# Squared ReLU of an MLP's first product: which engines do it

## The chip, the cores and the metric

The kernel runs on one core of a Trainium2 chip. The metric is the device time of one execution in microseconds, lower is better. A core has five engines that run side by side, each through its own instructions in order: TensorE (PE; PEld is its loading of weights), VectorE (DVE), ScalarE (ACT), GpSimd (POOL) and SyncE (SP), whose queue here issues all loads and stores. An instruction waits until what it needs is there, and everything behind it on its engine waits too.

## The reference, cut to what matters

Two layers of a flow-matching backbone run over 1,152 tokens (1,024 grid tokens and 128 context tokens) of 1,024 features. Each layer has a group of mixers with one output projection, and then an MLP of 4,096 hidden features:

```python
h2 = rms_norm(x, p['norm2']) * (1 + sc2) + sh2
x = x + g2 * (jnp.square(jax.nn.relu(h2 @ p['w1'])) @ p['w2'])
```

The vectors sc2, sh2 and g2 come from a modulation of the condition vectors, `silu(cond) @ w_mod + b_mod`, which each layer has for itself. All is float32.

## The kernel before, in words

Features lie on partitions, tokens in the free dimension. Products are made in two float32r parts (a high part, rounded, and the rest), by three matmuls for each pair of tiles, lines 1081 to 1083. The MLP's two products are done by blocks, two by two, with seven products in place of eight (Strassen and Winograd). Tokens are cut into four blocks of 288 (`BLK`), two for each half `q`; the hidden features are cut into 16 pairs `j` of tiles. One call of `Line.add` is one product of blocks of the first MLP product: 16 pairs by 2 halves make 32 of them a layer. Each is seven runs of 12 matmuls of 128x288, 84 in all.

`Line.products` writes the runs into PSUM banks. Run 0 goes into `bA`, which ScalarE copies into a bank `bB`. Run 1 goes into `bE`, which ScalarE copies to SBUF as `s5` (the trace calls it `s`). Run 2 is added into `bB`, which is copied into a bank `bC`. Run 3 is added into `bA`, which gives block c11; run 4 into `bB`, which gives c22; run 5 into `bC`, which gives c12; run 6 into `bB` again, which gives c21. So run 6 may start only when c22 has been read out of `bB`. `Line.add` weaves the last three runs of one product under the first four of the next: 0, 4 of the one before, 1, 5 of the one before, 2, 6 of the one before, 3.

What becomes of the four blocks is in `hidden`. The functions `c1` (c11 and c21) and `c2` (c22 and c12, to which `s5` is still to be added) take each block out of PSUM into a tile `hr`, square the positive part, and `keep` stores it to DRAM (`hd`), from where the second product loads it. `s5` and `hr` are from one pool of five buffers. The helpers `act` (line 208, ScalarE), `ptt` (190, GpSimd), `vtt` (193, VectorE) and `vstt` (205, VectorE) issue one instruction each, so the trace shows their lines.

The left operands are made as they are needed, by `Weights.version`: VectorE forms sums of weight tiles (`wl`, lines 187 and 193), ScalarE rounds them (`ws`, line 181), and GpSimd, or VectorE for some, takes the rest (`ws`, lines 184 and 187). A ring holds seven such tiles, and one is made when one is free.

In the first layer VectorE also makes the modulation vectors of the second (`mod_tile`, line 270): 48 tiles, with six reductions each, emitted after the steps 6 to 31 of the first MLP product (`MLP_MODS`). Their operands `wm` are loaded by SyncE's queue.

The instructions of each engine are put in order by a planner that simulates the program when it is built (`schedule_with_timeline_sim=True`). An order on paper is thus also a result of the costs that this simulation gives to each instruction, which are not those of the chip.

Of the kernel before, what the change touches and what calls it, by code (L numbers as in the profile page):

```python
# [42 lines left out]
# a block of tokens: a quarter of the grid and one of the context  # L43
# [16 lines left out]
def weave(main, n_main, side, n_side):  # L60
    """Emits two streams evenly interleaved, by their numbers of steps."""
    done = [0, 0]
    gens = [main, side]
    n = [max(n_main, 1), max(n_side, 1)]
    live = [True, True]
    while live[0] or live[1]:
        i = 0 if live[0] and (not live[1] or done[0] * n[1] <= done[1] * n[0]) else 1
        try:
            next(gens[i])
            done[i] += 1  # L70
        except StopIteration:
            live[i] = False


def weave_steps(main, n_main, side, n_side):
    """The main stream, with the steps of a side stream spread over its own."""
    done = 0
    for i in range(n_main):
        if next(main, END) is END:
            return  # L80
        while done * n_main < (i + 1) * n_side and next(side, END) is not END:
            done += 1
        yield
    yield from main


def weave_at(main, side, counts):
    """The main stream, with the given number of steps of a side stream after each of its own."""
    for n in counts:
        next(main, END)  # L90
        run_out(take(side, n))
    run_out(main)
# [6 lines left out]
def steps(n, span, i):  # L99
    """How many of n steps fall on i when they are spread over a span."""  # L100
    a, b = (n * min(max(i + e - span[0], 0), span[1] - span[0]) // (span[1] - span[0]) for e in range(2))
    return b - a
# [15 lines left out]
def build(ctx, tc, I, O):  # L118
# [9 lines left out]
    def urgent(gen, offset):  # L128
        """A stream whose instructions go before those around it."""
        while True:  # L130
            with tc.high_priority(offset):
                step = next(gen, END)
            if step is END:
                return
            yield step

    # pools that come and go
# [20 lines left out]
    def phase(st, tag, bufs, w=NW, side="left"):  # L158
        """A pool of [128, w] tiles for one phase of a layer."""
        pool = st.enter_context(tc.tile_pool(name=tag, bufs=bufs, side=side, reuse_waits="tile"))  # L160
        return lambda name, dt=F32: pool.tile([P, w], dt, tag=tag, name=name)

    def two_phases(st, tag, n1, n2, w):
        """The same in two places, by turns n1 and n2 tiles."""
# [72 lines left out]
    # the early columns apart from the others, which come later  # L237
# [18 lines left out]
    # adaLN vectors, feature on partitions: mod[l][:, j, cond]  # L256
# [3 lines left out]
    def mod_tile(l, j, piece):  # L260
        """mod[l][:, j] from the rows of w_mod's transpose, in pieces."""
# [19 lines left out]
    def segs(n):  # L281
        # (lo, hi, cond) within chunk n
        if n < NCH - 1:
            return [(0, NW, 0)]
        return [(0, NW - TP, 0), (NW - TP, NW, 1)]

    def rms_sums(xs, n, alone=False):
        """The sums over the feature tiles of the squares of chunk n."""
# [14 lines left out]
    def rms_scale(sq, ps, w=P):  # L303
        """1/rms of 3w tokens, to be turned."""
# [11 lines left out]
    def rms_turn(R, ps, w=P):  # L316
        """1/rms of 3w tokens on all partitions, in SBUF."""
# [16 lines left out]
    class HT:  # L334
        """Normalised and modulated activations in two float32r parts, [k][n]."""
# [49 lines left out]
    def weight(src):  # L385
        """The float32r parts of a [128, 8, 128] weight tile, as functions of its k."""
        p = [half(src, i) for i in range(2)]
        return tuple((lambda k, j=j: p[k // 4][j][:, ti(k % 4)]) for j in range(2))
# [15 lines left out]
    def project_tokens(l, group, ht, evac, s_):  # L404
        """256 features projected with the tokens on partitions, 128 tokens a step."""
# [16 lines left out]
    def store_mix(t, dst, n, g_):  # L422
        """The float32r parts of a chunk of 128 features of the mixers' output, to DRAM."""
# [7 lines left out]
    class B:  # L431
        """The arrays of one pair of heads, in chunks of 384 tokens."""
# [23 lines left out]
    # where the first layer's later modulation vectors are computed, of 32  # L456
    MODS = (10, 11, 11, 0)
    # the projections under the recurrences of the heads
# [5 lines left out]
    class HGRN:  # L464
        """The recurrence of one pair of heads.

        levels(g): the scores of chunk g's three blocks of 128 tokens, by the levels of a binary tree;
        tail(g): its state updates, and all but the backward states' part of its output;
        back(): the backward states, their part of the output and its norm, in reversed order.
        """  # L470
# [205 lines left out]
    def hgrns(pairs):  # L676
        """Both pairs of heads: the end of each part runs under the levels of the next."""
# [10 lines left out]
    RG_STEPS = 1 + 2 * 7  # L688

    def rglru(l, i, xa, gel, gw, ud, g_):  # L690
# [13 lines left out]
        # each function of ScalarE for both directions at once  # L704
# [53 lines left out]
    def split_q(ps, n, h_t, l_t, sub):  # L758
        # queries in the order (row half, column block, row, column) and scaled
# [20 lines left out]
    def qk_project(l, p, win, ht, qd, kd, s_, ns=range(NCH)):  # L780
# [9 lines left out]
        def evac_k(n, ps):  # L790
            # the grid's rows in pairs, by columns
# [12 lines left out]
    # the grid's upper half for all pairs of heads, then the context's tokens and the lower half  # L804
# [4 lines left out]
    # where the output projection is done, by the tokens' half: of the first features, of the last  # L809
# [3 lines left out]
    def attention(l, qd, kd, vd, pool, out):  # L813
        """All query tiles of the four pairs of heads.

        Yields once the first pair's operands are under way, then after each tile the one that is complete.
        """
# [169 lines left out]
    class Ends:  # L987
        """What becomes of the fifth product and of the four blocks of a product of blocks."""
# [4 lines left out]
    def lo_subs(n):  # L993
        """The engines of a version's seven subtractions, n of them on VectorE."""
        return iter([vsub if (i + 1) * n // 7 > i * n // 7 else psub for i in range(7)])

    class Weights:
        """The left operands of the seven products, version by version, in the order of their use."""
# [56 lines left out]
    class Line:  # L1055
        """Products of blocks one after the other, the end of each under the start of the next."""
# [53 lines left out]
    def pieces(b):  # L1110
        """Block b of tokens by chunks and conditions: (chunk, from, to, condition, place in the block)."""
# [4 lines left out]
    def half_of(q, t, d, load):  # L1116
        """Moves blocks 2q and 2q + 1 of a [128, 2 * BLK] tile from or to DRAM."""
# [14 lines left out]
    def load_blocks(srcs, q, new):  # L1132
        """Blocks 2q and 2q + 1 of two tiles of features."""
# [12 lines left out]
    def blocks_of(t):  # L1146
        """The two blocks of a tile, and both."""
        return [t[:, c * BLK:(c + 1) * BLK] for c in range(2)] + [t]

    def load_half(src, q, new):  # L1150
        """Blocks 2q and 2q + 1 of a tile of features."""
# [15 lines left out]
    class NormOperands:  # L1167
        """The right operands of the seven products, from the features 2i and 2i + 1 of half q of the tokens.

        The steps take 2, 4, 4 and 4 places of [128, 2, BLK] (the second after the first, the fourth after the  # L1170
        others).
        """
# [12 lines left out]
        def normed(self, k):  # L1185
            """Normalised and modulated in place."""
# [31 lines left out]
    def hidden_operands(hd, g, q, i, new_x, new):  # L1218
        """The right operands of the seven products, from the hidden features 2i and 2i + 1 of group g."""
# [30 lines left out]
    def small_parameters():  # L1250
        # forget-gate lower bounds: cumsum of the softmax over layers, less its first entry
# [17 lines left out]
        # log a = r * ca with ca = -8 softplus(-lambda); softplus by an atanh series, all [128, 4]  # L1269
# [25 lines left out]
    for l in range(DEPTH):  # L1295
# [28 lines left out]
        if l == 0:  # L1324
            # the modulation vectors arrive k by k: the scales on VectorE, the shifts on TensorE
# [98 lines left out]
        # A's recurrence under B's projections  # L1424
# [20 lines left out]
        def v_project(g):  # L1445
            c = slice(g * 2 * P, (g + 1) * 2 * P)

            def e(i, ps):
                s = ft("vs")[:, :2 * P]
                (acopy if i % 2 else vcopy)(s, ps)  # L1450
                if i < NC - 1:
                    # the grid's rows in pairs, by columns
# [30 lines left out]
        def u_parts(t, src, view):  # L1483
            """The float32r parts of some of the mixers' output."""
# [31 lines left out]
        # the first tiles of the attention under the last projections  # L1516
# [4 lines left out]
        # C's attention under the output projection, by halves of the tokens  # L1521
        h_st, x4_st = ExitStack(), ExitStack()
        if l:
            # the same places as in the first layer
# [54 lines left out]
        def middle():  # L1579
            """The norm of the first half of the tokens, and the first operands of the MLP from it."""  # L1580
# [33 lines left out]
        # MLP: each product of blocks, two by two, by Strassen's and Winograd's seven  # L1614
# [37 lines left out]
        def hidden(j, q):  # L1652
# [7 lines left out]
            def c1(r, ps):  # L1660
                t = ft("hr")[:, :BLK]
                act(t, ps, AF.Relu)
                ptt(t, t, t, ALU.mult)
                keep(r, 0, t)

            def c2(r, ps):
                t = ft("hr")[:, :BLK]
                vtt(t, ps, on.s5, ALU.add)
                vstt(t, t, 0.0, t, ALU.max, ALU.mult)
# [60 lines left out]
        def second(g, m, q):  # L1730
            def add(k, c, ps):
                """x += gate * product, on block c of q."""
# [59 lines left out]
def host_inputs(inp):  # L1792
# [17 lines left out]
    # blocks (output, input) = (0, 0), (0, 1), (1, 1), (1, 0) of the MLP's weights  # L1810
# [32 lines left out]
    # relative-position bias laid out per query tile; masked places hold a constant  # L1843
# [63 lines left out]
```

## Time and profile before

| | us |
|---|---|
| median of 3 runs | 3368.74 |
| lowest, highest | 3367.22, 3373.05 |
| span of the profiled execution | 3359.0 |
| first MLP product, first layer | about 840 to 1290 |
| first MLP product, second layer | about 2490 to 2890 |

The profiled execution has no whole time of its own on record beside its span, from its first instruction to its last. The median of the runs lies 9.7 us above the span. In the rows, times are counted from the span's start. A group's row gives line, engine, operation, the tile written and those read, the shape, the count, busy us, the mean of one in ns, and the idle time of the engine before them with what ended it. A wait's row says which engine and line stood for which, the sum in us, how often, and the longest.

### The profile page before, as it was taken

The page shows a single profiled execution, that of the slowest core. Times are in us where ns is not written, and L with a number is a line of the kernel's source. Part 1 is how long each engine was busy: PE and PEld are TensorE (multiplying, and loading weights), DVE is VectorE, ACT ScalarE, POOL GpSimd, SP SyncE. Part 2 cuts the span into 40 slices and gives each one's busy share as a digit, 9 for nine tenths or more (in the row PEclk, how much of TensorE's full clock was granted, in tenths as well). Part 3 has the DMA queues.
Part 4 walks back from the last instruction along what each step waited for, and adds up shares of the span by engine and source line. Part 5 has one row for each costly group of instructions (what it writes and reads, how often), then busy time and mean ns, then how long its engine had stood idle before and what let it go on. Part 6 is the DMA issues. An engine that isn't in the chain of part 4 may idle for free. (4 is left out here: it accounts for less than half of the span.)

```text
span 3359.0 us, 62376 instructions
## 1 busy us (share of the span) xinstructions
PE 2987.9 (89%) x21196; PEld 2829.2 (84%) x21196; DVE 2627.3 (78%) x6417; ACT 1535.1 (46%) x3878; POOL 1735.7 (52%) x1822
## 2 busy tenths in 40 slices
PE   7888998898788888898878899999988999899885
PEld 7877987797788888898878789988878999888885
DVE  7799964678999998999996687345878324899997
ACT  5453234554432225554555533455635333555445
POOL 4541222444744437777765311334546555777776
PEclk8999999999899989999999999999989999999997
DMA  7332449973355555322232212689644333532222
GB/s 269 83 115 89 135 117 272 262 244 114 116 164 159 154 163 171 96 85 89 73 117 67 57 31 78 185 245 289 193 130 122 109 105 106 166 98 86 89 73 73
DMA packets 391070, 452.26 MB, mean 135 GB/s; under 512 B 68192, under 2 KB 293600, under 8 KB 390752
## 3 DMA queue, kind: packets, MB, share of 16 engines
q1 hardware_dynamic: 390752, 448.28, 44.5%
q8 instruction: 168, 2.75, 0.3%
q14 instruction: 150, 1.23, 0.1%
HBM read 339.34 MB, written 108.79 MB: 133 GB/s over the span
## 5 line engine op out<-in xcount | busy, mean ns | idle before, releaser
L184 POOL TENSOR_TENSOR wl<-wr,wh 128x512 fp32r<-128x512 f32 x164 | 226.8, 1388 | 476.6 <-ACT wh L181 380.2
L184 POOL TENSOR_TENSOR ws<-wl,ws 128x512 fp32r<-128x512 f32 x160 | 230.6, 1445 | 231.6 <-ACT ws L181 223.5
L1081 PE MATMUL bB<-t,ws 128*128 128x288 f32 x768 | 240.6, 313 | 73.0 <-DVE hr L193 68.3
L1081 PE MATMUL bB<-T,wt 128*128 128x288 f32 x768 | 240.8, 314 | 67.7 <-ACT bB L181 51.0
L184 POOL TENSOR_TENSOR wt<-wl,wt 128x256 fp32r<-128x256 f32 x296 | 253.0, 862 | 68.7 <-ACT wt L181 65.3
L392 PE MATMUL pj<-hh,wh 128*128 128x384 f32 x640 | 221.5, 351 | 21.4 <-DVE vb L178 7.3
L1082 PE MATMUL bB<-t,ws 128*128 128x288 f32 x768 | 236.3, 308 | 1.0 <-DVE t L187 1.0
L1083 PE MATMUL bB<-t,ws 128*128 128x288 f32 x768 | 236.6, 308 | 0.0
L270 DVE CUSTOM_DVE_ANT_0 junk<-wm,sil,ma 128x384 bf16<-128x384 f32 (+1 forms) x320 | 230.0, 719 | 6.7 <-DMA wm<-in_w_mod 1.9
L1082 PE MATMUL bB<-T,wt 128*128 128x288 f32 x768 | 233.9, 305 | 0.0
L1083 PE MATMUL bB<-T,wt 128*128 128x288 f32 x768 | 232.9, 303 | 0.0
L394 PE MATMUL pj<-hh,wl 128*128 128x384 f32 x640 | 222.4, 348 | 4.2 <-POOL wl L184 4.2
L393 PE MATMUL pj<-hh,wh 128*128 128x384 f32 x640 | 222.9, 349 | 3.4 <-DVE hh L205 3.4
L1081 PEld LDWEIGHTS bB<-t,ws 128*128 128x128 f32 x768 | 153.5, 200 | 81.1 <-DVE hr L193 74.8
L1081 PEld LDWEIGHTS bB<-T,wt 128*128 128x128 f32 x768 | 150.5, 196 | 82.0 <-ACT bB L181 60.6
L184 POOL TENSOR_TENSOR wt<-wr,wt 128x256 fp32r<-128x256 f32 x210 | 184.4, 881 | 60.8 <-ACT wt L181 52.2
L184 POOL TENSOR_TENSOR T<-xb,T 128x288 fp32r<-128x288 f32 x192 | 180.6, 950 | 42.7 <-ACT T L181 42.1
L187 DVE TENSOR_TENSOR xb<-xb 128x288 f32<-128x288 f32 x288 | 190.8, 667 | 11.5 <-POOL B L184 6.3
L181 ACT CAST ws<-wl 128x512 fp32r<-128x512 f32 x160 | 98.7, 620 | 194.8 <-PE bB L1083 91.2
L181 ACT CAST T<-xb 128x288 fp32r<-128x288 f32 x256 | 110.3, 432 | 165.8 <-DVE xb L187 147.3
L1081 PE MATMUL bA<-B,wt 128*128 128x288 f32 x512 | 158.6, 310 | 26.7 <-DVE x L205 23.7
L205 DVE SCALAR_TENSOR_TENSOR x<-bB,mod,x 128x256 f32<-128x256 f32 (+2 forms) x576 | 169.7, 339 | 12.5 <-PE bB L1083 11.5
(336 smaller groups left out, 11474.7 us busy)
## 6 DMA issues: line engine op xcount, KB each, us to landing
wr<-in_w SPq DMA_DIRECT2D x308, 256.0 KB, 3.0
hd<-hr SPq DMA_DIRECT2D x256, 144.0 KB, 2.6
wm<-in_w_mod SPq DMA_DIRECT2D x160, 192.0 KB, 2.7
wr<-in_w_in SPq DMA_DIRECT2D x104, 256.0 KB, 3.1
bi<-in_bias SPq DMA_DIRECT2D x96, 192.0 KB, 4.3
QS<-qd SPq DMA_DIRECT2D x72, 256.0 KB, 4.2
xb<-hd SPq DMA_DIRECT2D x128, 144.0 KB, 2.2
xb<-hd SPq DMA_DIRECT2D x64, 288.0 KB, 2.8
```

The source lines that it names most:

```text
L181: nc.scalar.copy(out=out, in_=in_)
L184: nc.gpsimd.tensor_tensor(out=out, in0=a, in1=b, op=ALU.subtract)
L187: nc.vector.tensor_tensor(out=out, in0=a, in1=b, op=ALU.subtract)
L205: nc.vector.scalar_tensor_tensor(out=out, in0=a, scalar=s, in1=b, op0=op0, op1=op1)
L270: nc.vector.tensor_tensor_reduce(out=junk[:, :w], in0=r[:, :w], in1=sil[:, c, k0:k0 + w], scale=1.0, scalar=acc[c], op0=ALU.mult, op1=ALU. ...
L392: mm(ps, lhsT=wh(k), rhs=ah(k), start=k == first, stop=False)
L393: mm(ps, lhsT=wh(k), rhs=al(k), start=False, stop=False)
L394: mm(ps, lhsT=wl(k), rhs=ah(k), start=False, stop=k == last)
L1081: mm(ps, lhsT=w[:, 0, ti(i)], rhs=t[:, 0], start=start and i == 0, stop=False, skip_group_check=True)
L1082: mm(ps, lhsT=w[:, 0, ti(i)], rhs=t[:, 1], start=False, stop=False, skip_group_check=True)
L1083: mm(ps, lhsT=w[:, 1, ti(i)], rhs=t[:, 0], start=False, stop=i == n - 1, skip_group_check=True)
```

## The change

In `c1` the square of the ReLU's output moves from GpSimd's product to ScalarE's Square. In `c2` the addition of `s5` stays on VectorE; the one VectorE instruction behind it that took the maximum with 0 and multiplied becomes two on ScalarE, Relu and Square, both in place on the tile. The rest of the diff takes comments and docstrings out.

```diff
             def c1(r, ps):
                 t = ft("hr")[:, :BLK]
                 act(t, ps, AF.Relu)
-                ptt(t, t, t, ALU.mult)
+                act(t, t, AF.Square)
                 keep(r, 0, t)
 
             def c2(r, ps):
                 t = ft("hr")[:, :BLK]
                 vtt(t, ps, on.s5, ALU.add)
-                vstt(t, t, 0.0, t, ALU.max, ALU.mult)
+                act(t, t, AF.Relu)
+                act(t, t, AF.Square)
                 keep(r, 1, t)
```

## Rows read from the trace of the kernel before

**Rows 1.** The page's head: span, then busy time of each engine.

```profile
span 3359.0 us, 62376 instructions
PE 2987.9 (89%) x21196; PEld 2829.2 (84%) x21196; DVE 2627.3 (78%) x6417; ACT 1535.1 (46%) x3878; POOL 1735.7 (52%) x1822
```

**Rows 2.** Two stretches: length, busy us of PE, PEld, DVE, ACT, POOL; granted clock.

```profile
930.00:1265.00 335.00, 289.13 (x2000) 284.97 (x1999) 320.75 (x734) 99.32 (x213) 160.00 (x130) 0.93 0.53 158
...
2600.00:2850.00 250.00, 248.19 (x1860) 247.96 (x1859) 88.09 (x151) 90.17 (x194) 132.89 (x118) 0.99 0.35 106
```

**Rows 3.** Waits in 930:1265, then 830:930, then 2480:2600: us, times, longest.

```profile
PE bB L1081 <- DVE hr L193: 45.9, 17, 4.8
...
PE bB L1081 <- DVE hr L193: 9.3, 4, 4.2
...
PE bB L1081 <- DVE hr L193: 8.1, 3, 4.6
```

**Rows 4.** Timeline of 1119:1125, one wait of TensorE.

```profile
1119.21 0.39 ACT L181 COPY bC<-bB 128x288 f32<-128x288 f32 x1
...
1121.51 0.46 DVE L193 TENSOR_TENSOR hr<-bB,s 128x288 f32<-128x288 f32 x1
...
1122.02 0.40 PE L1081 MATMUL bB<-t,ws 128*128 128x288 f32 x1 [3.37 <-DVE hr L193]
...
1122.41 0.46 DVE L205 SCALAR_TENSOR_TENSOR hr<-hr 128x288 f32<-128x288 f32 x1
...
1124.51 0.45 DVE L193 TENSOR_TENSOR hr<-bC,s 128x288 f32<-128x288 f32 x1
1124.88 0.48 DVE L270 CUSTOM_DVE_ANT_0 junk<-wm,sil,ma 128x256 bf16<-128x256 f32 x1
```

**Rows 5.** VectorE in 930:1265, by line and shape: count, busy us, mean ns.

```profile
L270 DVE CUSTOM_DVE_ANT_0 junk<-wm,sil,ma 128x384 bf16<-128x384 f32 x92 | 79.1, 860 | 1.6
L270 DVE CUSTOM_DVE_ANT_0 junk<-wm,sil,par 128x384 bf16<-128x384 f32 x92 | 75.1, 816 | 1.5
L270 DVE CUSTOM_DVE_ANT_0 junk<-wm,sil,ma 128x256 bf16<-128x256 f32 x93 | 61.3, 660 | 1.7
L205 DVE SCALAR_TENSOR_TENSOR hr<-hr 128x288 f32<-128x288 f32 x48 | 31.6, 658 | 0.1
L187 DVE TENSOR_TENSOR ws<-wr,ws 128x512 fp32r<-128x512 f32 x14 | 15.0, 1070 | 1.0 <-ACT ws L181 1.0
...
L187 DVE TENSOR_TENSOR wl<-wr,wl 128x512 f32<-128x512 f32 x13 | 13.7, 1055 | 0.0
```

**Rows 6.** GpSimd in 930:1265, the product that the change moves.

```profile
L190 POOL TENSOR_TENSOR hr<-hr 128x288 f32<-128x288 f32 x49 | 44.1, 904 | 44.8 <-ACT hr L208 42.6 <-DMA wr<-in_w 1.9
```

**Rows 7.** Shortest/median/longest ns, from lines 270 and 187 and tile hr.

```profile
L270 DVE CUSTOM_DVE_ANT_0 junk<-wm,sil,par x160: 589/617/1661, 116.2 to 1240.9; 128x384 bf16<-128x384 f32 x160
...
L187 DVE TENSOR_TENSOR ws<-wr,ws x52: 673/692/1792, 828.5 to 2874.7; 128x512 fp32r<-128x512 f32 x52
...
L205 DVE SCALAR_TENSOR_TENSOR hr<-hr x128: 441/458/4008, 844.3 to 2884.0; 128x288 f32<-128x288 f32 x128
```

**Rows 8.** ScalarE in 700:1400 by shape, then its line 208 in the whole run.

```profile
L208 ACT ACTIVATE sq<-x 128x288 f32<-128x288 f32 x29 | 12.3, 439 | 19.0 <-DVE x L205 13.9 <-DVE sq L193 5.1
...
L208 ACT ACT_TABLE_LOAD  x35: 1283/1283/1283, 0.7 to 2176.5; - x35
```

**Rows 9.** Timeline of TensorE, 2708:2714, first matmuls of two runs.

```profile
2708.44 0.29 PE L1081 MATMUL bA<-t,ws 128*128 128x288 f32 x1
...
2713.20 0.29 PE L1081 MATMUL bE<-t,ws 128*128 128x288 f32 x1
```

**Rows 10.** Tile hr alone in two starts: busy us of VectorE, ScalarE, GpSimd.

```profile
840.00:930.00 90.00, 15.72 (x20) 3.85 (x10) 10.45 (x11) 0.89 0.41 122
...
2490.00:2600.00 110.00, 18.73 (x24) 5.08 (x13) 11.12 (x13) 0.91 0.46 132
```

**Rows 11.** What the queue of loads and stores waited for, 930:1265.

```profile
SPq L211 <- DVE hr L205: 41.7, 34, 2.8
```

## The prediction, made before the change was run

> **What bounds the kernel now.** I read the page's head first: TensorE is busy for most of the span and VectorE for 78% of it [rows 1]. These are means over stages, so the next view is the busy time by stretches, cut at the first and last instructions on tile hr, the only tile that the change touches. The two layers differ [rows 2]. In the second layer, from 2600 to 2850, TensorE issues 1860 matmuls in 250 us with the clock granted at 0.99, which is 2.4 GHz almost throughout. At 84 matmuls a product this is 11.3 us a product; VectorE is busy for 88 us of the 250. TensorE is the bound there. In the first layer, from 930 to 1265, it issues 2000 in 335 us, 23.8 products at 14.1 us each, and VectorE is busy for 320.8 us of the 335, or 96%. VectorE is the bound there, because line 270 is in its queue too [rows 5].
>
> The waits show how VectorE holds TensorE [rows 3]: 45.9 us in 17 waits for the addition that takes c22 out of bank bB. The timeline shows one of them [rows 4]: the addition starts at 1121.51, with other work of VectorE straight before and behind it, and TensorE, 3.37 us idle, goes on at 1122.02. The other loss is clock: 0.93 granted in this stretch against 0.99 in the other [rows 2]. At the second layer's pace 23.8 products would take 23.8 x 11.3 = 269 us. So at most 335 - 269 = 66 us can be won in this stretch by taking work off VectorE.
>
> **What is removed from VectorE.** 128 instructions of line 205 go, 64 a layer. Alone one takes 458 ns (the median [rows 7]), but in the stretch the mean is 658 ns over 48 of them [rows 5]. The next instruction starts before the last has ended: one of 0.45 us started at 1124.51 and the next at 1124.88 [rows 4], so 0.08 us of each is covered, and 48 x 0.58 = 28 us come free.
>
> **What is removed from GpSimd.** 49 products of 904 ns in the stretch, 44.1 us of its 160 us busy [rows 2, 6]. GpSimd itself is not the bound (160 of 335), so its own time is worth nothing. But VectorE's instructions with two operands in SBUF are much longer in this stretch than their medians: line 270 at 128x384 has a median of 617 ns and a longest of 1661, and means of 816 and 860 here; the 54 sums of 128x512 have a median near 690 ns and means of 1.04 to 1.08 us [rows 5, 7]. The excess is 92 x (0.860 - 0.617) + 92 x (0.816 - 0.617) = 41 us, 93 x (0.660 - 0.48) = 17 us for the 128x256 (0.48 is the one shown in the timeline [rows 4]), and 54 x 0.37 = 20 us: 77 us. That GpSimd makes this excess is argued, not shown by one row. If it does so in proportion to its busy time, the share of the moved products is 44.1 / 160 = 28%, or 21 us. The bounds are 0 (the excess has another cause) and 44 us (every moment of those products held VectorE). I take 21, the proportional share, since the other 72% of GpSimd's work stays.
>
> The Trainium skill says why it could be so: SBUF — State Buffer, "Who interferes with whom", has VectorE and GpSimd share one pair of ports under an exclusive lock, which a VectorE instruction with two SBUF inputs needs. The trace agrees as far as the stretched means go; by the rule at its hardest, every overlap blocks, it would be the upper bound of 44.
>
> **What is added to ScalarE.** 64 Square for c1 and 64 Relu and 64 Square for c2 a layer. No Relu from SBUF is in the trace; the nearest row is Square of 128x288 from SBUF, 439 ns [rows 8], and I take it for all. In the stretch this is (49 + 2 x 48) x 0.44 = 64 us on top of 99.3, 163 of 335: no bound. In the second layer it is six a product, 2.6 us, on top of 90.2 us for 22.1 products (4.1 us each): 6.7 of 11.3. There the cover is the distance between the end of run 3 and the next write of bank bE, where the Relu of c11 has to be done: run 3 starts at 2708.44 and takes half of the 24 matmuls on bA, to about 2710.0, and run 1 of the next product starts at 2713.20 [rows 9]. So 3.2 us of slack, against a Square and a cast ahead of it, about 1.1 us. I cost the second layer's middle at 0; with the cover gone it would cost up to 2.6 us a product, 58 us.
>
> **The wait that is added.** ScalarE's Relu of c2 now waits for VectorE's addition. Behind it on ScalarE stand the copies of bE and bB that TensorE needs, and the casts of the weights, on which GpSimd waits. In the case shown the addition for c12 ran at 1124.51, while the copy into bC had already been done at 1119.21 [rows 4]. If the Relu goes ahead of that copy, the copy ends at about 1124.96 + 2 x 0.44 + 0.39 = 1126.2, and TensorE, which went on at 1122.02 and has three runs of 1.6 us before it needs the bank, asks for it at 1126.8. It just holds. I put the hand-over at half of a Relu and a Square a product, 0.5 us, 12 us for the stretch; the bounds are 0 and four of the added instructions, 1.76 x 23.8 = 42 us.
>
> The stores move with it. SyncE's queue stood 41.7 us for line 205's results [rows 11], with the loads of wm and of the weights behind. The store of c2 now waits for two instructions on ScalarE, about 0.9 us behind the addition, in place of one on VectorE that starts 0.9 us after it or later (1121.51, 1122.41 [rows 4]). I cost this at 0, since those loads' waits are not what VectorE stood for; the same row, 41.7 us, bounds it above.
>
> **Sum.** In the stretch VectorE has 320.8 - 28 - 21 = 272 us of work left. Its idle 14 us stay, and 12 us of hand-over come: 298, against a floor of 269. Gain 37 us. In the first layer's start (840 to 930) ten instructions of line 205 go: tile hr cost VectorE 15.7 us there, of which ten additions of 0.45 are 4.5 [rows 10]. TensorE stood 9.3 us for the additions [rows 3]; I take half, 5 us, as other work of that start stays. In the second layer's start 18.7 - 5.4 = 13 us go and TensorE stood 8.1 [rows 3, 10]: 4 us. The joints to the second product, where all engines are part busy, count 0. Sum 37 + 5 + 4 = 46 us: a span of 3359 - 46 = 3313, and with the 9.7 us between the span and the median of the runs, 3323 us.
>
> **Rivals.**
> *TensorE becomes the bound everywhere* (more relief than I take, hand-over 0): 66 us in the stretch and half to all of the two starts' 17 us, 75 to 83 us: about 3290. For it: 320.8 - 28 - 44 = 249 is below the floor. Against: products and VectorE's work would have to fit without any wait. Chance 0.10.
>
> *The hand-over eats the gain.* ScalarE now moves in step with VectorE, and where VectorE waits for a cast (some of the weights' rests are VectorE's, the 1.0 us of waits in the row of ws [rows 5]) the two wait in turn. With no relief from GpSimd and 28 us less 12 to 28 of hand-over, 0 to 20 us are left with the starts: about 3358. Chance 0.17.
>
> *Slower: ScalarE's queue stands behind c22.* The planner puts the Relu of c22 right behind its addition as the simulation sees it, but on the chip VectorE is late (TensorE alone waited up to 4.8 us for it [rows 3]). The casts of weights and two copies stand behind; if they become what TensorE waits for, each product pays a cast, GpSimd's rest of it (mean near 1.45 us), Relu, Square and copy, some 3.3 us in a row, 79 us. It decides when the hold is over (28 + 21 + 9) / 23.8 = 2.4 us a product; at 3.3 the time is 3368.7 + 79 - 58 = 3390. Against: the ring holds seven weight tiles ahead. The Trainium skill speaks for this side: ScalarE: Activation LUTs, "Rules for kernel authors", gives relu and mul to VectorE rather than ScalarE. Here one instruction of 458 ns alone becomes two of 439, which agrees, but on an engine with idle time. Chance 0.12.
>
> *Tables.* If Relu and Square were not in one loaded table, each pair would cost a load of 1283 ns, at least 128 x 1.28 = 164 us slower, about 3530. Against: the last table load of the run starts at 2176.5, while ScalarE's Squares and Relus of the second MLP come after it [rows 8]. Chance 0.01.
>
> **Chances.** The forecast has the remaining 0.60, over 20 to 65 us of gain, 3304 to 3349. About 0.2%, 6.7 us, is what a measurement of this kernel can tell from no change. The second rival falls for 0.10 above it and 0.07 within, the slower one for 0.02 within: faster 0.60 + 0.10 + 0.10 = 0.80, same 0.09, slower 0.11. The range of 3296 to 3365 leaves out most of the slower side, part of the second rival's poor end and half of the first.
>
> **What would show it.** Right: in the first layer's stretch line 205 on hr gone, the means of line 270 nearer 617 ns, TensorE's waits for the addition well under 45.9 us, and some 12.5 us a product; the second layer's middle unchanged at 11.3. Wrong: waits of TensorE for ScalarE's copies or for weights in place of those for VectorE, means of line 270 as before, or the second layer's middle slower. What would make the number wrong above all is another order from the planner.

## The result, and the profile after

The changed kernel takes 3323.98 us (median of 4 runs, 3319.91 to 3330.52); the kernel before 3367.98. The ratio is 0.9874, with a 95% interval of 0.9857 to 0.9892: 1.3% faster. A second measurement of the same program, beside other experiments, gave 0.9887 [0.9872, 0.9902]. The forecast was 3323.

The page's head after the change, which answers to [rows 1]:

```profile
span 3322.5 us, 62536 instructions
PE 2954.7 (89%) x21196; PEld 2793.0 (84%) x21196; DVE 2535.4 (76%) x6289; ACT 1680.9 (51%) x4262; POOL 1617.0 (49%) x1694
```

VectorE has 92 us less to do and GpSimd 119 us less; ScalarE has 146 us more. The span is 36.5 us shorter. Where, shows best between two events that both traces have: the start of ScalarE's Relu of c11 in the first and in the 32nd product of blocks. The busy time of the engines between them, first layer and then second, for the kernel before:

```profile
838.68:1287.41 448.73, 381.67 (x2604) 374.10 (x2604) 421.30 (x893) 153.92 (x335) 233.99 (x186) 0.92 0.50 149
2502.65:2879.79 377.14, 359.97 (x2619) 356.69 (x2618) 193.56 (x301) 153.72 (x335) 217.42 (x186) 0.97 0.37 111
```

and for the kernel after:

```profile
842.07:1257.86 415.79, 365.75 (x2607) 354.40 (x2607) 370.13 (x831) 219.23 (x522) 175.57 (x125) 0.98 0.55 162
2473.55:2839.47 365.92, 351.97 (x2616) 349.67 (x2615) 152.46 (x239) 228.84 (x521) 164.61 (x125) 0.99 0.39 115
```

(The columns are length, then busy us of TensorE, its weight loads, VectorE, ScalarE and GpSimd, the granted clock, the DMA engines' share and GB/s.) The first layer's product is 32.9 us shorter, the second's 11.2; together 44.1. The rest of the span is 7.6 us longer. TensorE's part of the first layer's 32.9 is of two kinds. Its idle time falls from 448.7 - 381.7 = 67 to 415.8 - 365.8 = 50 us. And the same matmuls (2604 and 2607) take 381.7 and 365.8 us, with the clock granted at 0.92 before and 0.98 after. So about half of the 32.9 us is less idle time, and half came with the clock.

In the stretch with line 270, which answers to [rows 2], and in the two behind it:

```profile
930.00:1205.00 275.00, 241.27 (x1733) 232.51 (x1733) 265.58 (x655) 126.01 (x305) 101.77 (x69) 0.99 0.59 175
1205.00:1265.00 60.00, 57.27 (x431) 56.95 (x430) 30.64 (x52) 41.16 (x100) 27.73 (x25) 1.00 0.46 141
2560.00:2800.00 240.00, 240.00 (x1812) 240.00 (x1811) 64.53 (x102) 142.60 (x320) 93.79 (x73) 1.00 0.36 105
```

1733 matmuls in 275 us are 20.6 products at 13.3 us, where they were at 14.1. VectorE is still busy for 97% of it, and then for half of the 60 us behind it. The second layer's middle runs without a gap at 11.1 us a product. The waits of 930:1205, for [rows 3]:

```profile
ACT hr L208 <- DVE hr L193: 143.8, 41, 6.0
...
PE bB L1081 <- DVE hr L193: 25.6, 19, 2.1
...
PE bB L1081 <- ACT bC L181: 7.6, 15, 1.3
...
PE bA L1083 <- POOL ws L184: 0.4, 1, 0.4
```

ScalarE now stands 144 us for VectorE's additions. Little of that shows at TensorE: it waits 7.6 us for the copy into bC, for which it did not wait from 930 to 1265 before, and 0.4 us for GpSimd's rests. TensorE's waits for the additions are as many but short, 2.1 us at most in place of 4.8. VectorE's groups in the same stretch, for [rows 5]:

```profile
L270 DVE CUSTOM_DVE_ANT_0 junk<-wm,sil,ma 128x384 bf16<-128x384 f32 x91 | 74.4, 818 | 3.3 <-DMA wm<-in_w_mod 1.1
L270 DVE CUSTOM_DVE_ANT_0 junk<-wm,sil,par 128x384 bf16<-128x384 f32 x90 | 69.6, 773 | 1.6
L270 DVE CUSTOM_DVE_ANT_0 junk<-wm,sil,ma 128x256 bf16<-128x256 f32 x91 | 65.9, 724 | 4.0 <-DMA wm<-in_w_mod 1.9
...
L187 DVE TENSOR_TENSOR wl<-wr 128x512 f32<-128x512 f32 x12 | 11.5, 959 | 0.0
L193 DVE TENSOR_TENSOR wl<-wr 128x512 f32<-128x512 f32 x11 | 10.8, 979 | 0.0
...
L187 DVE TENSOR_TENSOR wl<-wr,wl 128x512 f32<-128x512 f32 x11 | 8.7, 787 | 0.0
...
L187 DVE TENSOR_TENSOR ws<-wr,ws 128x512 fp32r<-128x512 f32 x9 | 6.1, 683 | 0.0
```

Two things are to be seen. The stretch holds nearly as much of line 270 as the 335 us did before (91 in place of 92 of a kind), with three products fewer beside it. And line 270's means have hardly moved (818, 773 and 724 ns after 860, 816 and 660), while of the weights' sums and rests of 128x512, all at 1.04 to 1.08 us before, the rests on VectorE are at their median again (683), one group of sums is nearer to it (787), and two have come down little (959 and 979). The new instructions and the table loads on ScalarE, in the whole run, for [rows 8]:

```profile
L208 ACT ACTIVATE hr<-hr x384: 425/445/457, 843.7 to 2847.6; 128x288 f32<-128x288 f32 x192
...
L208 ACT ACT_TABLE_LOAD  x35: 1283/1283/1283, 0.7 to 2148.5; - x35
```

They cost 445 ns each, and no table load was added (35 before and after). The stores' wait on SyncE's queue in 930:1205, 41.7 us before [rows 11], is now:

```profile
SPq L211 <- ACT hr L208: 10.5, 19, 1.2
```

### The profile page after: what moved, and what is told of

Read it like the earlier page. It is cut to its first block, busy times and chain, and to the rows that moved or that the text cites. A ratio compares the mean times of both kernels' runs of the same rounds, so it can differ in the third digit from the quotient of the medians.

```text
span 3322.5 us, 62536 instructions
## 1 busy us (share of the span) xinstructions
PE 2954.7 (89%) x21196; PEld 2793.0 (84%) x21196; DVE 2535.4 (76%) x6289; ACT 1680.9 (51%) x4262; POOL 1617.0 (49%) x1694
## 5 line engine op out<-in xcount | busy, mean ns | idle before, releaser
L1081 PE MATMUL bB<-t,ws 128*128 128x288 f32 x768 | 235.7, 307 | 48.9 <-DVE hr L193 41.1
L208 ACT ACTIVATE hr<-hr 128x288 f32<-128x288 f32 x384 | 169.5, 444 | 197.1 <-DVE hr L193 190.6
L270 DVE CUSTOM_DVE_ANT_0 junk<-wm,sil,ma 128x384 bf16<-128x384 f32 (+1 forms) x320 | 234.9, 734 | 11.1 <-DMA wm<-in_w_mod 5.3
L1082 PE MATMUL bB<-t,ws 128*128 128x288 f32 x768 | 230.9, 301 | 2.1 <-DVE t L187 2.1
L1083 PE MATMUL bB<-t,ws 128*128 128x288 f32 x768 | 230.9, 301 | 0.0
```

Of the source, the lines that this page charges most:

```text
L208: nc.scalar.activation(out=out, in_=in_, func=f, **kw)
L270: nc.vector.tensor_tensor_reduce(out=junk[:, :w], in0=r[:, :w], in1=sil[:, c, k0:k0 + w], scale=1.0, scalar=acc[c], op0=ALU.mult, op1=ALU. ...
L1081: mm(ps, lhsT=w[:, 0, ti(i)], rhs=t[:, 0], start=start and i == 0, stop=False, skip_group_check=True)
L1082: mm(ps, lhsT=w[:, 0, ti(i)], rhs=t[:, 1], start=False, stop=False, skip_group_check=True)
L1083: mm(ps, lhsT=w[:, 1, ti(i)], rhs=t[:, 0], start=False, stop=i == n - 1, skip_group_check=True)
```

## The experiments

Each was timed against the kernel before in five rounds. "First to last" is the time from the first to the 32nd c11, first layer and second.

| kernel | us | ratio, interval | first to last, us | VectorE busy in the first layer's |
|---|---|---|---|---|
| before | 3367.98 | | 448.7, 377.1 | 421.3 |
| the change | 3323.98 | 0.9874 [0.9857, 0.9892] | 415.8, 365.9 | 370.1 |
| c1 only | 3333.84 | 0.9888 [0.9873, 0.9903] | 422.4, 368.8 | 397.1 |
| c2 only | 3351.61 | 0.9939 [0.9927, 0.9952] | 432.8, 370.3 | 397.6 |
| the change, GpSimd loaded | 3350.56 | 0.9938 [0.9924, 0.9951] | 426.7, 372.9 | 385.7 |
| the change, weights' sums on GpSimd | 3367.58 | 0.9994 [0.9984, 1.0005] | 454.9, 365.1 | 367.7 |
| before, no line 270 here | 3297.40 | 0.9793 [0.9778, 0.9809] | 375.2, 375.4 | 193.8 |
| the change, no line 270 here | 3281.00 | 0.9735 [0.9713, 0.9757] | 364.2, 366.8 | 151.0 |
| the change, 12 tiles later | 3330.07 | 0.9891 [0.9876, 0.9906] | 406.3, 364.9 | 317.9 |
| c1 only, 12 tiles later | 3346.60 | 0.9942 [0.9927, 0.9957] | 414.1, 369.6 | 345.4 |
| the change, tiles held to their places | 3315.72 | 0.9843 [0.9824, 0.9862] | 402.5, 365.7 | 375.7 |
| before, tiles held | 3358.52 | 0.9979 [0.9965, 0.9993] | 433.5, 374.7 | 420.0 |
| c1 only, tiles held | 3327.50 | 0.9882 [0.9867, 0.9896] | 410.9, 371.2 | 395.3 |
| the change, again | 3328.86 | 0.9887 [0.9872, 0.9902] | 416.1, 365.7 | 369.6 |

**Only c1.** Against the kernel before:

```diff
                 act(t, ps, AF.Relu)
-                ptt(t, t, t, ALU.mult)
+                act(t, t, AF.Square)
                 keep(r, 0, t)
```

> Only c1 is changed: its square goes from GpSimd to ScalarE; c2 keeps its one instruction on VectorE. Theory A (the gain is VectorE's own instructions of line 205): VectorE keeps all its work, line 270's means stay at 0.82 to 0.86 us for 128x384, time 3358 to 3368, a gain of 0 to 10 us. Theory B (GpSimd's products held VectorE, as the prediction's 21 us of relief say): line 270's means fall by some 28% of their excess, 0.06 us, time 3345 to 3352.

It took 3333.84 us, 1.1% less: more than either theory gave it. VectorE's own program is the same, and yet it is busy for 24 us less between the marks:

```profile
839.29:1261.69 422.40, 370.22 (x2609) 362.51 (x2608) 397.13 (x893) 180.15 (x398) 178.47 (x125) 0.95 0.54 159
```

GpSimd's products did hold VectorE, as theory B says. But line 270 isn't where it shows. Line 205, which is still there, is. First the kernel before, then this run, each between its own marks:

```profile
L270 DVE CUSTOM_DVE_ANT_0 junk<-wm,sil,ma 128x384 bf16<-128x384 f32 x96 | 83.6, 871 | 1.6
...
L205 DVE SCALAR_TENSOR_TENSOR hr<-hr 128x288 f32<-128x288 f32 x62 | 45.1, 728 | 0.2
```

```profile
L270 DVE CUSTOM_DVE_ANT_0 junk<-wm,sil,ma 128x384 bf16<-128x384 f32 x96 | 84.9, 884 | 2.5 <-DMA wm<-in_w_mod 0.8
...
L205 DVE SCALAR_TENSOR_TENSOR hr<-hr 128x288 f32<-128x288 f32 x62 | 35.0, 565 | 0.3
```

Ten of the 24 us are there, and the weights' sums and rests give most of the others.

How the holding works can be read from the timeline, instruction by instruction. In the kernel before, one of c1's products and one instruction of line 205:

```profile
1125.42 1.08 POOL L190 TENSOR_TENSOR hr<-hr 128x288 f32<-128x288 f32 x1 [4.78 <-ACT hr L208]
1125.89 0.92 DVE L205 SCALAR_TENSOR_TENSOR hr<-hr 128x288 f32<-128x288 f32 x1
```

VectorE's instruction starts inside GpSimd's, takes twice its 0.46 us, and ends 0.31 us behind GpSimd's. This is the rule in that trace. Of line 270's 276 reductions that start from 930 to 1265, 78 are over 15% longer than they are alone (0.617 and 0.48 us). Of these 78, 77 start inside an instruction of GpSimd and one 0.03 us ahead of one; they end after GpSimd's end by their own length less 0.2 us. Six others start inside one too, all in its last 0.23 us, and are not stretched; of the 193 that start while GpSimd does nothing, 192 are not. Of the 78, 25 are held by c1's products, for 8.7 us in all, and 53 by the weights' rests, for 48.8. In the changed kernel's 930:1205 the 25 are gone, but the rests hold line 270 57 times, for 54.8 us, beside three products fewer. That is why its means stayed.

**Only c2.** Against the kernel before:

```diff
                 vtt(t, ps, on.s5, ALU.add)
-                vstt(t, t, 0.0, t, ALU.max, ALU.mult)
+                act(t, t, AF.Relu)
+                act(t, t, AF.Square)
                 keep(r, 1, t)
```

> Only c2 is changed: its maximum and product go from VectorE to two instructions on ScalarE; c1's square stays on GpSimd. Theory A (line 205 is the gain): nearly all of it, 3324 to 3334. Theory B (GpSimd's products held VectorE): about half, 3340 to 3350, with line 270's means above 0.82 us.

3351.61 us, 0.6% less: 1.6 us above theory B's range, and far from theory A's. VectorE is busy for 397.6 us between the marks, as in the run with c1 alone, and the first layer is still 10 us longer than there:

```profile
843.92:1276.68 432.76, 376.03 (x2604) 364.59 (x2603) 397.62 (x831) 194.23 (x460) 233.10 (x186) 0.95 0.53 155
```

VectorE is idle for 35 us here and for 25 there; why was not traced. The two parts give 1.1% and 0.6% alone, and 1.3% and 1.1% together in two measurements. On top of c1, c2 gives nothing that these times can tell, though in the traces the two products are 6 to 7 and 3 us shorter with it.

**GpSimd loaded for nothing.** Against the changed kernel, in c1, with `load` a tile of ones:

```diff
                 act(t, t, AF.Square)
+                for _ in range(2):
+                    ptt(load, load, load, ALU.mult)
                 keep(r, 0, t)
```

> The changed kernel with two products of 128x128 of constants on GpSimd beside each c1, read by nobody: GpSimd's load comes back, nothing waits for it but GpSimd's own later work. Theory A: 3322 to 3330. Theory B (GpSimd's activity stretches VectorE's instructions with two operands in SBUF): 3336 to 3350, with line 270's means higher than in the changed kernel (0.82, 0.80 and 0.72 us).

3350.56 us: 27 us of the gain are gone, though nobody reads the products. GpSimd's group between the marks:

```profile
L190 POOL TENSOR_TENSOR load<-load 128x128 f32<-128x128 f32 x94 | 59.2, 630 | 3.9
```

VectorE is busy for 385.7 us in place of 370.1:

```profile
844.65:1271.31 426.66, 366.74 (x2598) 354.93 (x2597) 385.70 (x831) 219.22 (x522) 231.44 (x219) 0.97 0.53 157
```

This run puts load on GpSimd alone, so it shows the cause by itself: what GpSimd does stretches VectorE. How much of the 27 us comes that way it doesn't show: the first layer's product is 10.9 us longer, the second's 7.0, and the rest lies outside the two. What it did not leave alone is GpSimd's own order, in which the weights' rests now stand behind the products; this run does not part the two.

**Weights' sums on GpSimd.** Against the changed kernel, for the first layer's first product (`pool` is true there):

```diff
-            vtt(s1, a22, a21, ALU.add)
+            (ptt if pool else vtt)(s1, a22, a21, ALU.add)
...
-            vsub(s4, a12, s2)
+            (psub if pool else vsub)(s4, a12, s2)
```

> The changed kernel with the sums of weights of the first layer's first product (line 187 and 193 on wl, 75 of 128x512, 66.6 us on VectorE) on GpSimd. Theory A (VectorE's queue is still the bound in the first layer, 97% busy in the stretch with line 270): VectorE has 66 us less, products with line 270 among them go from 13.35 to about 11.5 us, 3285 to 3300. Theory B (each instruction of GpSimd holds VectorE, 0.6 to 0.9 us): line 270's means rise by 0.2 us, the gain is given back, 3315 to 3345.

3367.58 us: the whole gain of the change is given back, beyond theory B's range. 75 sums, 66.6 us, left VectorE, and its busy time fell by 2.4 us, because line 270 rose again (to 958, 892 and 833 ns from 818, 721 and 796) and the rest with it:

```profile
L270 DVE CUSTOM_DVE_ANT_0 junk<-wm,sil,ma 128x384 bf16<-128x384 f32 x96 | 92.0, 958 | 3.1 <-DMA wm<-in_w_mod 0.4
L270 DVE CUSTOM_DVE_ANT_0 junk<-wm,sil,ma 128x256 bf16<-128x256 f32 x96 | 85.6, 892 | 5.2 <-DMA wm<-in_w_mod 2.4
L270 DVE CUSTOM_DVE_ANT_0 junk<-wm,sil,par 128x384 bf16<-128x384 f32 x96 | 80.0, 833 | 2.9 <-DMA wm<-in_w_mod 0.7
```

VectorE's work is not the whole of the loss, though. It is busy for 367.7 us of 454.9 here, and idle for 87 us in place of 46. TensorE's waits for the copy into bC rose from 7.6 to 20.1 us between the marks, and VectorE's for ScalarE's casts from 3.0 to 28.0:

```profile
846.44:1301.30 454.86, 380.51 (x2611) 370.48 (x2610) 367.69 (x755) 221.94 (x522) 281.11 (x201) 0.93 0.50 149
```

```profile
DVE ws L187 <- ACT ws L181: 28.0, 9, 4.9
...
PE bB L1082 <- ACT bC L181: 20.1, 11, 4.7
```

The sums now come from GpSimd, at 1.43 us each, and the casts need them. This run does not part what these slower sums cost from what the stretching costs.

**Without line 270 in the first product.** Against the kernel before and against the changed one:

```diff
-    mod = [C.tile([P, 48, 2], F32, name=f"mod{l}") for l in range(DEPTH)]
+    mod = [C.tile([P, 48, 2], F32, name="mod0")] * DEPTH
...
-                elif not last:
-                    for _ in range(steps(48, MLP_MODS, n - 1)):
-                        mod_tile(l + 1, next(later), sqt)
```

> The kernel before, leaving out the second layer's modulation vectors (48 tiles of line 270 in the first layer's first product; the second layer takes the first layer's vectors). If VectorE's queue with line 270 is what holds the first layer, it now runs as the second layer does (377 us from first to last c11 in place of 449): 3295 to 3310. If something else sets the first layer's pace, above 3340.

> The changed kernel with the same left out. If the gain comes from VectorE's queue, only what the starts of the two layers give is left of it, some 11 us a layer: 20 to 24 us below the kernel before with the same left out, about 3275 to 3287. If the gain does not hang on line 270, the whole of it stays, 40 us or more between the two, about 3255 to 3265.

Both kernels leave out the second layer's modulation vectors, and the second layer takes the first layer's. 3297.4 and 3281.0 us. The first layer now runs as the second does, before and after:

```profile
846.42:1221.61 375.19, 356.00 (x2610) 353.10 (x2609) 193.75 (x301) 154.22 (x336) 219.42 (x186) 0.98 0.38 112
2437.26:2812.61 375.35, 357.21 (x2618) 354.02 (x2617) 193.29 (x301) 153.77 (x336) 217.01 (x186) 0.98 0.38 112
```

```profile
847.61:1211.86 364.25, 352.18 (x2605) 349.98 (x2604) 150.99 (x239) 229.10 (x521) 165.33 (x125) 0.98 0.39 115
2436.83:2803.61 366.78, 355.10 (x2617) 353.29 (x2616) 152.94 (x239) 228.53 (x521) 164.14 (x125) 0.98 0.40 115
```

The change is worth 11 and 9 us in the two products then, and 16 us of the medians, in place of 44; the forecast for this was 20 to 24, and the second kernel's runs spread from 3265.6 to 3287.1. So line 270 is the condition for the larger part of the gain. The smaller part comes from the starts of the products, in both layers alike: 9.4 of the 11 us up to the 7th c11, and 8.9 us up to the 9th in the second layer. With line 270 its loads of wm went too (the DMA engines' share fell from 0.50 to 0.38), and these two runs do not part the loads from VectorE's work. What points to the work is that TensorE's longest waits are for VectorE's additions [rows 3].

**Twelve tiles later.** Against the changed kernel: the loop in the first layer's product makes 36 tiles, and the second layer's mixer stage the other 12, for which the condition vectors are loaded again.

```diff
...
-        left = iter(range(16, 48 if l == 0 else 16))
+        left = iter(range(16 if l == 0 else 36, 48))
...
-                    for _ in range(steps(48, MLP_MODS, n - 1)):
+                    for _ in range(steps(36, MLP_MODS, n - 1)):
```

> The changed kernel with 12 of the 48 modulation tiles made later, in the second layer's mixer stage, where VectorE has idle time. Theory A (VectorE's queue still sets the first layer after the change, 97% busy): 56 us less there, products with line 270 below 12.5 us, 3298 to 3314. Theory C (it is ScalarE's wait for VectorE's additions, 144 us in that stretch, that now sets the pace): little gained, 3318 to 3335, products at 13 us or more.

> The same with c2 kept on VectorE's one instruction, and only c1's square on ScalarE. Theory A: VectorE has 35 us more to do in the first layer, 5 to 12 us slower than the run above. Theory C: without ScalarE's wait it is no slower, or some us faster.

3330.07 us: no gain, and within theory C's range. The first layer's product is 9.5 us shorter, but the part of the span between the two products grew from 1215.7 to 1238.2 us. The trace of the product tells more. The tiles end at 1134 in place of 1207, and products are as slow as in the changed kernel up to there, 13.5 us from c11 to c11, and fast from there on:

```profile
1050.00:1100.00 50.00, 45.45 (x321) 44.06 (x320) 48.71 (x117) 23.93 (x58) 19.81 (x14) 0.97 0.57 171
1100.00:1150.00 50.00, 44.67 (x326) 43.27 (x326) 36.90 (x95) 24.21 (x58) 19.01 (x15) 1.00 0.55 166
1150.00:1200.00 50.00, 50.00 (x379) 50.00 (x379) 13.34 (x23) 29.10 (x65) 14.51 (x12) 1.00 0.34 100
```

So fewer tiles do not thin the queue; they only end sooner. How dense they stand beside a product is the planner's choice. With c2 on VectorE the same kernel takes 3346.6 us, 16.5 more: no sign that ScalarE's wait for VectorE sets the pace (theory C), as it should then be no slower.

**Tiles held to their places.** This tests what the last run suggests. Against the changed kernel, the kernel before, and the one with c1 alone:

```diff
-MLP_MODS = (6, 32)
+MLP_MODS = (4, 31)
...
-                vtt(t, ps, on.s5, ALU.add)
+                added[0] = vtt(t, ps, on.s5, ALU.add)
...
-                        mod_tile(l + 1, next(later), sqt)
+                        with tc.issue_after(added[0].ins):
+                            mod_tile(l + 1, next(later), sqt)
```

(`vtt` returns its instruction here; `issue_after` fixes the order on VectorE. The tiles also begin two steps earlier.)

> The changed kernel with the 48 modulation tiles held to their places: each queued on VectorE behind the last addition emitted before it, and emitted after the steps 4 to 30 in place of 6 to 31. Theory D (the planner filled the time freed on VectorE with modulation tiles, so that the products beside them stayed at 13.35 us and the last five ran with VectorE half idle): spread over all products, VectorE's 370 us need some 12 us a product, first to last c11 385 to 400 us in place of 416, 3295 to 3310. Rival (VectorE's total sets the time however it is spread, or ScalarE's wait for the additions does): 3318 to 3330.

> The kernel before with the same places. Theory D: VectorE was busy for 421 of 449 us there, so spreading can give at most some 20 us: 3350 to 3366. If spreading alone gives 25 us or more, most of the change's gain was a matter of order: below 3343.

> Only c1 changed, c2 on VectorE as before, with the same places. VectorE has 397 us to do: 12.8 us a product, 10 to 20 us slower than the first run of this call if line 205 costs what its rows say (35 us); the same time if what c2 frees is not what counts.

> The changed kernel itself, on the same chip as the three above, to compare them with: 3320 to 3328.

The changed kernel with the tiles held takes 3315.72 us, 0.9843 [0.9824, 0.9862] of the kernel before; the changed kernel beside it 0.9887. It is the fastest version of this study that leaves nothing out. It lies between the two ranges, above theory D's 3310 and below the rival's 3318:

```profile
842.54:1245.08 402.54, 365.86 (x2617) 356.83 (x2616) 375.68 (x831) 218.86 (x521) 178.22 (x125) 0.97 0.56 166
```

The first layer's product is 13 us shorter with 5 us more of VectorE's work: it is the spread that counts. From the 7th c11 to the 30th a product takes 12.2 us, as theory D said; the last two, which have tiles beside them now, take 28.2 us together in place of 23.3. The kernel before, so held, gains 0.2%. Its product is 15 us shorter, but the part of the span between the two products is 9 us longer. With c1 alone it is 0.9882: here c2's move is worth 12 us (3327.5 to 3315.7), and 8 us of the first layer's product:

```profile
841.01:1251.88 410.87, 365.98 (x2618) 359.38 (x2618) 395.33 (x887) 178.66 (x395) 175.89 (x124) 0.96 0.55 162
```

What c2 frees on VectorE is worth something, then, but without the holding the planner fills it with tiles.

## Why the prediction was right, and where its steps were off

*VectorE is the bound in the first layer.* Shown, with the reserve on the loads of wm: without line 270 there, 28 of the 44 us of the gain are gone.

*28 us from line 205: mis-sized.* The prediction took 48 instructions at 0.58 us. Four pairs of runs differ by c2 alone (before and c2 only, c1 only and the change, and the two pairs with later and with held tiles). VectorE's busy time between the marks differs by 23.7, 27.0, 27.5 and 19.6 us for 62 instructions, so 0.32 to 0.44 us each, or 15 to 21 us for the 48. That is about what one takes alone, 0.46 less the 0.08 that is covered. The step that failed is the use of the stretched mean: what line 205 was held for is not freed with it, since GpSimd then holds the next instruction. The prediction counted this time as line 205's, though it had itself put such time down to GpSimd.

*21 us of relief from GpSimd.* With c1 alone, 24.2 us less for 61 products, or 19 for the stretch's 49: the size was right. So was the mechanism, since load on GpSimd alone lengthens VectorE's work, and the timeline shows it instruction by instruction. A product of 0.92 us held VectorE by 24.2 / 61 = 0.40 us on average, not by its whole length, so the upper bound of 44 was not met. The Trainium skill (SBUF — State Buffer, "Who interferes with whom") has one rule for the two engines' shared ports, an exclusive lock. The trace agrees: the stretched instructions of VectorE end only behind GpSimd's. What was wrong is where I looked for the relief: the prediction said that line 270's means would come nearer to 617 ns, and they stayed. With c1 alone the relief was on line 205 itself and on the weights' sums and rests. Of the two parts of the change the one on GpSimd, whose own time I had called worth nothing, gave the larger gain.

*12 us for the hand-over.* TensorE stood 7.6 us for the copy into bC. The slower rival needed the casts behind ScalarE's waits to become what TensorE waits for. They didn't: its waits for GpSimd's rests, which need these casts, are 0.4 us in the same stretch.

*12.5 us a product in the stretch: this step failed.* It was 13.3. The step kept the tiles of line 270 as dense as before, but the order is the planner's, and it put the same tiles beside three products fewer. Fast products behind the last tile gave part of it back. From the 7th c11 to the 30th, before and after:

```profile
940.06:1263.90 323.84, 279.42 (x1929) 275.49 (x1928) 310.76 (x716) 94.21 (x203) 152.71 (x124) 0.93 0.53 159
```

```profile
936.66:1234.58 297.92, 265.44 (x1918) 256.92 (x1917) 273.33 (x662) 142.17 (x342) 111.81 (x77) 0.99 0.58 171
```

The gain was 25.9 us where the sum had 37. VectorE's work fell by 37.4 us, where the sum had 28 + 21 = 49. Its idle time rose from 13.1 to 24.6 us, by 11.5, where the sum kept it and put 12 of hand-over in its place. So the missing 11 us are mostly line 205's term. The 12 were about the right number for another reason: 15.2 of the 24.6 us of idle time lie behind the last tile, where TensorE is the bound.

*5 and 4 us for the starts: mis-sized.* They were 6.8 (to the 7th c11) and 11.0 us (to the 9th). I had priced the second start by half of TensorE's 8.1 us of waits. The same 668 matmuls there, before and after:

```profile
2502.70:2621.04 118.34, 101.17 (x668) 97.89 (x667) 103.92 (x141) 59.16 (x129) 79.23 (x62) 0.90 0.43 124
```

```profile
2473.50:2580.90 107.40, 93.45 (x668) 91.28 (x668) 84.50 (x125) 75.41 (x176) 64.69 (x46) 0.97 0.47 136
```

Of the 10.9 us between these marks, 7.7 are matmuls that ran at a higher granted clock (0.97 in place of 0.90), and 3.2 less idle time. So more was won than the waits' own length. That their going is what raised the clock is argued, not shown.

*9.7 us between span and median: wrong.* In the kernels run here a profiled execution lies about 2 us above its own span (3324.26 over 3322.5). By this the profiled execution of the kernel before took about 3361 (an estimate), one of its faster ones: its other runs lie at 3359 to 3375. By spans the change gave 36.5 us, and by medians 44. So that the total was met to 1 us is luck, by errors that cancel: 43.7 us from the stretch and the starts for the 46 of the sum, 7.6 us lost elsewhere in the span, and a median of before that lies that much above its profile. The 7.6 us (3.4 ahead of the first c11, the others behind it and outside the two products) were not traced. I take them as the spread between executions, which is not shown; the changed kernel run again had its first c11 another 2.5 us later.

## What to carry to other kernels

Before work is given to GpSimd because GpSimd is idle, look at what VectorE does at that moment: with VectorE full, each of GpSimd's products cost VectorE 0.4 us here, and moving 75 sums over cost the whole gain. Price what is taken off a full engine by its time alone, not by its stretched mean: the holding passes on to the next instruction. And where a planner orders the instructions, time freed on a full engine need not be spread over what needs it: find in the trace what has moved into it, and fix the order of the filler work by hand (0.4% here, for six lines).

## What the hardware showed

An instruction of VectorE with two operands in SBUF that started inside one of GpSimd's, other than in its last 0.23 us, stood until about its end (77 of line 270's 78 long ones), and one that started outside was not stretched (192 of 193). On average VectorE's busy time rose by 0.17 us for an instruction of GpSimd of 0.63 us (15.6 us over 94, constants of 128x128) and by 0.40 for one of 0.92 (c1's squares). For one of 1.43 (75 sums of 128x512) an estimate is 0.66: VectorE's work fell by 2.4 us where 75 x 0.69 = 52 us of sums, at their median, had left. These are averages over what the planner put beside them, in this kernel. That ScalarE could stand 144 of 275 us for another engine's results, at the head of the queue that empties TensorE's banks, and cost TensorE 7.6 us, I had not expected either.
